# Giving out the last part of a convolution norm as a line of stages over four channel tiles

## The chip, the cores and the metric

The kernel runs on one core of one Trainium2 chip. The metric is device time in microseconds of one execution; the runs of the kernel before are given as a median of three. A core has five engines that run side by side and meet through semaphores: TensorE (PE, matrix products; its weight loads are shown as PEld), VectorE (DVE), ScalarE (ACT), GpSimd (POOL) and SyncE (SP), which here mostly issues DMAs. Each engine works through its own queue in order: an instruction that waits holds up everything behind it on that engine.

## The reference

One inference step of a one-layer streaming encoder for a prompt of 2048 tokens and a sample of 64 tokens with a cache: an input projection, then a convolution module and a chunk-band attention on the same normalised input, a gated merge, an output projection, and a SwiGLU feed-forward part. What matters here is the convolution module:

```python
def layer_norm(x, g, b):
    xf = x.astype(jnp.float32)
    mu = jnp.mean(xf, axis=-1, keepdims=True)
    var = jnp.mean(jnp.square(xf - mu), axis=-1, keepdims=True)
    y = (xf - mu) * lax.rsqrt(var + NORM_EPS)
    return (y * g.astype(jnp.float32) + b.astype(jnp.float32)).astype(x.dtype)

def conv_module(u, hist, w_dw, b_dw, ln_g, ln_b, w_out):
    ext = jnp.concatenate([hist, u], axis=1)
    y = lax.conv_general_dilated(
        ext, w_dw[:, None, :], window_strides=(1,), padding='VALID',
        dimension_numbers=('NWC', 'WIO', 'NWC'), feature_group_count=CONV_DIM)
    y = jax.nn.silu(layer_norm(y + b_dw, ln_g, ln_b))
    return y @ w_out, ext[:, -(CONV_K - 1):]
```

`...` of the layer is left out: the projection with `w_out` and the merge come in the kernel's second phase. All is computed in float32 to the accuracy of products of split numbers: an operand x is held as a high part (x rounded to the format that PE multiplies) and a low part (x minus the high part), and a product is three matmuls.

## The kernel before

**Two phases.** The first phase goes through the 2112 tokens in four blocks (576, 512, 512 and 512 tokens; the first holds the 64 sample tokens). For each block PE computes the stages q, 0, k, 1, v, 2, 3, g in this order (line 564): q, k and v are projections, 0 to 3 are the four channel tiles of the convolution's GLU input, g are the gates. The second phase merges convolution and attention (`merge`, line 1736), projects, and does the feed-forward part.

**Side work in lanes.** Only PE's order is written out by hand (line 1644); side work is written as Python generators that are resumed between PE's products. `Stream` keeps an estimate of each engine's load; every 500 ns of estimated PE time (`STEP_NS`, line 37) a tick pumps the lanes: norms, `work`, attention, `tail`, convolution taps. A generator yields an estimated time (`stream.when("act")` is the time at which ACT's queue is estimated to be done), and is not resumed before PE's estimate has reached it. Each tick resumes the lane `tail` at most once. When stage 0 of the next block begins, and again at the end of the first phase, the lanes `conv` and `tail` are drained: what is left in them is given out at once, without its times (lines 1696 to 1698 and 1710 to 1712).

**The convolution norm.** `conv_norm` (line 1296) is the generator in the lane `tail`: one for the 64 sample tokens and one for 512 prompt tokens of block 0, then one of 512 tokens for each of the blocks 1 to 3. The two of block 0 run one behind the other. It works on `y`, four channel tiles of 128 partitions. POOL adds the four tiles to `s`, PE multiplies by a matrix of 1/512 (`total`, tile `pm`), DVE subtracts the mean, ACT squares, POOL adds, PE sums again, ACT takes the square root and DVE the reciprocal. Then comes the last part: POOL multiplies the four tiles by `s` (lines 1332 to 1334), and for each tile ACT computes a tanh into a temporary `ln`, DVE computes gain and bias in place on `y` and the product with 1 + tanh, ACT copies the high part, DVE subtracts to get the low part, and SP stores both to `c_d` in DRAM, from which the second phase loads them (tile `cin`).

**Buffers.** `temp` takes one of seven buffers of the ring "t", which gates, attention, the q and k rows and the norms share. `parts` takes a pair (part_h, part_l) of rings with two buffers each (`NS = 2`, line 781), which the norm shares with `store_kq` (q and k parts, line 1038) and `finish_head` (attention's output, line 1443). A pair is free when its store has landed. `low` (line 740) would give a subtraction to POOL if that were sooner by `TT_LESS`, which is 9e9 (line 43).

At the end of the first phase its pools are closed, and the second phase's pool of tiles (line 1720) takes the same memory: a tile there, such as `t` of `merge`, waits until the old tiles under it have been read.

Of the kernel before, what the change touches and what calls it, by code (L numbers as in the profile page):

```python
# [10 lines left out]
AF = mybir.ActivationFunctionType  # L11
# [99 lines left out]
class Lane:  # L111
# [18 lines left out]
    def step(self, entry):  # L130
        try:
            got = next(entry[0])
        except StopIteration:
            self.gens.remove(entry)
            return
        entry[1], entry[2] = got if isinstance(got, tuple) else (got, {})
# [486 lines left out]
def streaming_layer(ctx: ExitStack, tc: tile.TileContext, I, O):  # L623
    nc = tc.nc
    stream = Stream()
    pe, dve, act, gps = (
        Meter(e, n, stream) for e, n in ((nc.tensor, "pe"), (nc.vector, "dve"), (nc.scalar, "act"), (nc.gpsimd, "pool"))
    )
# [43 lines left out]
    lnh = const.tile([P, 8], F32, name="lnh")  # L672
# [67 lines left out]
    def low(hi, lo, src, n, less=0.0):  # L740
        e, name = either(n, less)
        stream.after(name, "act")
        e.tensor_tensor(lo, src, hi.bitcast(F32), ALU.subtract)
        return name
# [38 lines left out]
    def temp(name, shape=(P, 512)):  # L783
        return wk.tile(list(shape), F32, tag="t", name=name, bufs=NT)

    def parts(n=None, shape=(P, 512)):
        return (
            wk.tile(list(shape), F32R, tag="sh", name="part_h", bufs=NS),
            wk.tile(list(shape), F32R, tag="sl", name="part_l", bufs=NS),
        )  # L790
# [226 lines left out]
    bias = wk.tile([P, 640], F32, name="bias")  # L1017
# [278 lines left out]
    def conv_norm(y, c0, n, t0):  # L1296
        yv = y[:, :, c0 : c0 + n]
        yield lambda: not conv.gens
        s = wk.tile([P, 512], F32, tag="ln_s", bufs=1)

        def total():
            ps = ps_g.tile([P, 512], F32, tag="gp", name="pm")
            pe.matmul(ps[:, :n], ones, s[:, :n], start=True, stop=True)
            return ps

        gps.tensor_tensor(s[:, :n], yv[:, 0], yv[:, 1], ALU.add)
        for ct in (2, 3):
            gps.tensor_tensor(s[:, :n], s[:, :n], yv[:, ct], ALU.add)
        yield stream.when("pool") + PE_LAG
        pm = total()  # L1310
        yield stream.when("pe")
        for ct in range(4):
            dve.tensor_tensor(yv[:, ct], yv[:, ct], pm[:, :n], ALU.subtract)
        yield stream.when("dve")
        act.activation(s[:, :n], yv[:, 0], AF.Square)
        for ct in range(1, 4):
            tmp = temp("ln")
            act.activation(tmp[:, :n], yv[:, ct], AF.Square)
            yield stream.when("act")
            gps.tensor_tensor(s[:, :n], s[:, :n], tmp[:, :n], ALU.add)  # L1320
        yield stream.when("pool") + PE_LAG
        pm = total()
        yield stream.when("pe")
        act.activation(s[:, :n], pm[:, :n], AF.Sqrt, bias=eps_t)
        yield stream.when("act")
        for c in range(0, n, P):
            e = min(n, c + P)
            dve.reciprocal(s[:, c:e], s[:, c:e])
            yield
        yield stream.when("dve")  # L1330
        done = []
        for ct in range(4):
            gps.tensor_tensor(yv[:, ct], yv[:, ct], s[:, :n], ALU.mult)
            done.append(stream.when("pool"))
        for ct in range(4):
            yield done[ct]
            tmp = temp("ln")
            act.activation(tmp[:, :n], yv[:, ct], AF.Tanh, bias=lnh[:, 4 + ct : 5 + ct], scale=lnh[:, ct : ct + 1])
            yield stream.when("act")
            dve.tensor_scalar(yv[:, ct], yv[:, ct], lng[:, ct : ct + 1], lnb[:, ct : ct + 1], ALU.mult, ALU.add)  # L1340
            dve.scalar_tensor_tensor(tmp[:, :n], tmp[:, :n], 1.0, yv[:, ct], ALU.add, ALU.mult)
            yield stream.when("dve")
            hi, lo = parts()
            act.activation(hi[:, :n], tmp[:, :n], AF.Copy)
            yield stream.when("act")
            name = low(hi[:, :n], lo[:, :n], tmp[:, :n], n, TT_LESS)

            def store(ct=ct, hi=hi, lo=lo):
                for l, a in enumerate((hi, lo)):
                    nc.sync.dma_start(c_d[l, ct, :, t0 : t0 + n], a[:, :n].bitcast(F32))  # L1350

            stream.at(stream.when(name), store)

    def gates(b, free):

        o = PBLOCKS[b][0]
        w = PBLOCKS[b][1] - o

        def part(g, ws, c0, c1):
            ps = columns(*ws, kts(hh), kts(hl), c0, c1)  # L1360
            t = temp("gate")
            stream.after("act", "pe")
            act.activation(t[:, : c1 - c0], ps[:, : c1 - c0], AF.Tanh, scale=0.5)
            nc.scalar.dma_start(g_d[g // 8, g % 8, :, o + c0 : o + c1], t[:, : c1 - c0])

        def pair(g):
            ws = [W.get(("in", 2560 + g * P, h)) for h in range(2)]
            return [[[w[l][:, k, e * P : e * P + P] for w in ws for k in range(4)] for l in range(2)] for e in range(2)]

        n = 16 - SPLIT_G if b + 1 < len(PBLOCKS) else 16  # L1370
        for g in range(0, n, 2):
            for e, ws in enumerate(pair(g)):
                for c in halves(0, w):
                    part(g + e, ws, *c)
                if e:
                    W.done()
                    W.done()
                yield g + e
        rest = [ws for g in range(n, 16, 2) for ws in pair(g)]
        for c0, c1 in ((0, w // 2), (w // 2, w)):  # L1380
            for i, ws in enumerate(rest):
                part(n + i, ws, c0, c1)
                if c1 == w and i % 2:
                    W.done()
                    W.done()
            free["columns"] = c1
# [261 lines left out]
    for b, stage in ORDER:  # L1648
        lo, hi = PBLOCKS[b]
# [43 lines left out]
        else:  # L1693
# [7 lines left out]
            if stage == 3:  # L1701
                if b == 0:
                    tail.add(conv_norm(y, 0, SMP, 0))
                    tail.add(conv_norm(y, SMP + HIST, QB, SMP))
                else:
                    tail.add(conv_norm(y, 0, QB, lo))
# [675 lines left out]
```

## Time and profile before

| What | Value |
|---|---|
| Median of 3 runs | 2945.97 us (2940.69, 2946.77, 2945.97) |
| Profiled execution, its own time | 2941.67 us |
| Span of the profile | 2939.5 us |
| Mean granted clock of PE | 0.997 |
| First tanh to last part of the 64-wide norm, block 0 | 272.3 to 302.3 us |
| The same, block 1 | 550.3 to 579.5 us |

The span runs from the first to the last instruction. In rows of the timeline the columns are start (us from the span's start), duration in us, engine, source line, operation, tiles written <- tiles read, shape, count, and in brackets the idle time of the engine before and what ended it. All operations are recorded in one helper, so nearly all have line 105; tiles are told apart by their names. In rows by tile there stand duration in ns (least/median/most), then the start of the first and of the last of the group. The granted clock is the share of its full clock that PE was given.

### The profile page before, as it was taken

Reading aid. Unit: us, or ns where it says so; the run is one execution under the profiler, and the core shown is the slowest. Engines: PE = TensorE matmul, PEld = TensorE weight load, DVE = VectorE, ACT = ScalarE, POOL = GpSimd, SP = SyncE. Lnnn points to the kernel's source line nnn. Section 1 sums busy time; section 2 is a strip of 40 time slices with the busy share of each in tenths; the row PEclk is TensorE's granted clock in tenths of the full one; section 3 lists DMA queues with packets and bytes.
Section 4 is the critical chain, followed back from the end, with each engine's and each line's share of the span. In section 5 each row is a group of like instructions: output and inputs, shape, how many; then the busy total and the mean of one; then the engine's idle time right before and its main releaser. Section 6 shows DMA issues by size and latency. Waiting matters only on the chain.

```text
span 2939.5 us, 44832 instructions
## 1 busy us (share of the span) xinstructions
PE 2889.3 (98%) x16193; PEld 2587.5 (88%) x16193; DVE 2053.9 (70%) x3648; ACT 1362.7 (46%) x2453; POOL 1164.9 (40%) x753
## 2 busy tenths in 40 slices
PE   7999999999999999999999999999999999999999
PEld 5899777888888887988999998999999999999998
DVE  5897788668967885577777756666666557566666
ACT  3346543751564266563444345444444345444442
POOL 1201210111011002553566452366567742465667
PEclk9999999999999999999999999999999999999999
DMA  9989899978996987984444875332333965333333
GB/s 322 315 305 314 287 281 329 285 232 306 285 297 197 320 270 224 291 295 157 144 144 146 292 261 200 97 122 94 115 115 104 346 220 179 97 103 106 115 107 127
DMA packets 467067, 628.04 MB, mean 214 GB/s; under 512 B 36196, under 2 KB 314584, under 8 KB 466845
## 3 DMA queue, kind: packets, MB, share of 16 engines
q1 hardware_dynamic: 452944, 606.11, 63.4%
q10 hardware_dynamic: 13901, 19.08, 1.9%
q8 instruction: 127, 2.08, 0.3%
q14 instruction: 95, 0.78, 0.1%
HBM read 476.53 MB, written 148.54 MB: 213 GB/s over the span
## 4 chain that ended last, share of the span: by engine, by line
PE 47%; DVE 2%; ACT 1%; DMA 1%; issue 1%; POOL 0%; SPq 0%; ACTq 0%; DVEq 0%; POOLq 0%
PE ps L105 29%; PE pd L105 13%; PE pw L105 5%; DVE wlo L105 1%; ACT whi L105 1%; DVE ps L105 0%; DMA cin<-o_d 0%; DMA x<-x_d 0%; DVE acc L105 0%; ACT xn L105 0%; DMA wst<-in_w_ffn_in 0%; DMA wfo<-in_w_ffn_out 0%; DMA tg<-g_d 0%; DVE sums L105 0%; PE pt L105 0%
## 5 line engine op out<-in xcount | busy, mean ns | idle before, releaser
L105 PE MATMUL ps<-t,whi 128*128 128x384 f32 (+1 forms) x2112 | 502.0, 322 | 2.8 <-ACT u L105 1.7
L105 POOL TENSOR_TENSOR wlo<-wst,whi 128x1024 fp32r<-128x1024 f32 (+1 forms) x159 | 362.7, 2293 | 246.1 <-ACT whi L105 214.4
L105 ACT ACTIVATE whi<-wst 128x1024 fp32r<-128x1024 f32 (+1 forms) x265 | 258.3, 979 | 316.1 <-PE ps L105 129.6
L105 PE MATMUL ps<-b,whi 128*128 128x384 f32 (+1 forms) x1584 | 380.7, 325 | 6.4 <-DVE v L105 2.1
L105 PEld LDWEIGHTS ps<-t,whi 128*128 128x128 f32 x2112 | 367.8, 188 | 10.1 <-ACT u L105 3.9
L105 DVE SCALAR_TENSOR_TENSOR y<-u,wd,y 128x512 f32<-128x512 f32 (+1 forms) x480 | 370.1, 774 | 8.0
L105 PE MATMUL ps<-hh,whi 128*128 128x512 f32 (+2 forms) x992 | 362.8, 366 | 0.1
L105 DVE TENSOR_TENSOR acc<-acc,pd 128x512 f32<-128x512 f32 x482 | 322.2, 685 | 48.1 <-PE pd L105 45.6
L105 PE MATMUL ps<-hh,wlo 128*128 128x512 f32 (+2 forms) x992 | 345.2, 348 | 0.0
L105 PE MATMUL ps<-hl,whi 128*128 128x512 f32 (+2 forms) x992 | 344.5, 347 | 0.0
L105 PE MATMUL ps<-t,wlo 128*128 128x384 f32 (+1 forms) x1056 | 338.5, 321 | 0.0
L105 PE MATMUL pd<-whi,hid 128*128 128x512 f32 x912 | 297.9, 391 | 0.6 <-DVE hid L105 0.3
L105 PEld LDWEIGHTS ps<-b,whi 128*128 128x128 f32 x1584 | 276.9, 188 | 14.6 <-DVE v L105 3.2
L105 ACT ACTIVATE pr<-pr,sm 128x640 f32<-128x640 f32 (+3 forms) x272 | 201.9, 749 | 137.1 <-DVE sm L105 134.8
L105 PE MATMUL ps<-b,wlo 128*128 128x384 f32 (+1 forms) x792 | 256.1, 323 | 0.0
L105 POOL TENSOR_TENSOR r<-t,mhalf 128x1 f32<-128x1 f32 (+2 forms) x68 | 82.3, 1219 | 403.7 <-DVE t L105 377.8
L105 PEld LDWEIGHTS ps<-hh,wlo 128*128 128x128 f32 x992 | 186.5, 188 | 22.6
L105 DVE TENSOR_TENSOR wlo<-wst,whi 128x1024 fp32r<-128x1024 f32 (+1 forms) x106 | 135.9, 1286 | 100.3 <-ACT whi L105 98.9
L105 PEld LDWEIGHTS pd<-whi,hid 128*128 128x128 f32 x912 | 171.2, 188 | 37.2 <-DVE acc L105 1.8
L105 PEld LDWEIGHTS ps<-hh,whi 128*128 128x128 f32 x992 | 187.0, 189 | 18.2 <-issue 3.3
L105 PEld LDWEIGHTS ps<-hl,whi 128*128 128x128 f32 x992 | 187.4, 189 | 14.3 <-issue 1.7
L105 PEld LDWEIGHTS ps<-t,wlo 128*128 128x128 f32 x1056 | 198.2, 188 | 0.8
(233 smaller groups left out, 6309.6 us busy)
## 6 DMA issues: line engine op xcount, KB each, us to landing
whi<-w_din_h SPq DMA_DIRECT2D x72, 512.0 KB, 6.4
wlo<-w_din_l SPq DMA_DIRECT2D x72, 512.0 KB, 7.3
wst<-sum_d SPq DMA_DIRECT2D x131, 256.0 KB, 3.1
wfo<-in_w_ffn_out SPq DMA_DIRECT2D x64, 512.0 KB, 4.1
wmod<-in_w_ada SPq DMA_DIRECT2D x46, 512.0 KB, 8.8
sum_d<-ws SPq DMA_DIRECT2D x88, 256.0 KB, 2.0
wst<-in_w_ffn_in SPq DMA_DIRECT2D x85, 256.0 KB, 3.2
wst<-in_w_in SPq DMA_DIRECT2D x40, 512.0 KB, 6.0
```

The source lines that it names most:

```text
L105: self.last = f(*args, **kw)
```

## The change

After POOL's four products the code no longer finishes one tile before it begins the next. The work of a tile is three functions: `swish` (the tanh), `times` (DVE's two operations) and `give` (high part, low part, store). They are given out as a line: step i does `give` for tile i - 2, then `times` for tile i - 1, then `swish` for tile i, in six steps for the four tiles. Ahead of each step there is one `yield`: the later of POOL's estimate for tile min(i, 3) and, from the second step on, the later of the estimates of ACT and DVE. Before there were four resumptions for each tile, with a `yield` between copy and low part, which now come in one step. The temporaries of up to three tiles are held at once. The operations themselves are unchanged.

```diff
-        for ct in range(4):
-            yield done[ct]
-            tmp = temp("ln")
-            act.activation(tmp[:, :n], yv[:, ct], AF.Tanh, bias=lnh[:, 4 + ct : 5 + ct], scale=lnh[:, ct : ct + 1])
-            yield stream.when("act")
+        tmps = [None] * 4
+
+        def swish(ct):
+            tmps[ct] = temp("ln")
+            act.activation(tmps[ct][:, :n], yv[:, ct], AF.Tanh, bias=lnh[:, 4 + ct : 5 + ct], scale=lnh[:, ct : ct + 1])
+
+        def times(ct):
+            tmp = tmps[ct]
             dve.tensor_scalar(yv[:, ct], yv[:, ct], lng[:, ct : ct + 1], lnb[:, ct : ct + 1], ALU.mult, ALU.add)
             dve.scalar_tensor_tensor(tmp[:, :n], tmp[:, :n], 1.0, yv[:, ct], ALU.add, ALU.mult)
-            yield stream.when("dve")
+
+        def give(ct):
+            tmp = tmps[ct]
             hi, lo = parts()
             act.activation(hi[:, :n], tmp[:, :n], AF.Copy)
-            yield stream.when("act")
             name = low(hi[:, :n], lo[:, :n], tmp[:, :n], n, TT_LESS)
 
-            def store(ct=ct, hi=hi, lo=lo):
+            def store():
                 for l, a in enumerate((hi, lo)):
                     nc.sync.dma_start(c_d[l, ct, :, t0 : t0 + n], a[:, :n].bitcast(F32))
 
             stream.at(stream.when(name), store)
+
+        for i in range(6):
+            yield max(done[min(i, 3)], stream.when("act", "dve") if i else 0.0)
+            for step, ct in ((give, i - 2), (times, i - 1), (swish, i)):
+                if 0 <= ct < 4:
+                    step(ct)
```

## The prediction

> **What bounds the kernel now.** I read the page's first part, then who TensorE waited for, then the stretches around its two longest stops in the first phase.
>
> ```profile
> span 2939.5 us, 44832 instructions
> PE 2889.3 (98%) x16193; PEld 2587.5 (88%) x16193; DVE 2053.9 (70%) x3648; ACT 1362.7 (46%) x2453; POOL 1164.9 (40%) x753
> ...
> PE pt L105 <- DVE kn L105: 6.1, 2, 4.0
> PE ps L105 <- DVE t L105: 5.8, 5, 3.4
> ```
>
> TensorE (PE) is busy 98% of the span, so only what stops PE, or slows its clock, counts; the convolution norm runs on ACT, DVE and POOL and matters where PE waits behind it. PE's waits are few. The longest single wait in each of the two rows shown, 4.0 and 3.4 us, stands next to a convolution norm. In the table of stretches, the columns are length, then busy time of PE, weight loads, DVE, ACT and POOL, then granted clock and DMA:
>
> ```profile
> 355.00:360.50 5.50, 1.55 (x17) 0.64 (x8) 3.81 (x8) 2.85 (x7) 0.21 (x1) 1.00 0.59 159
> 360.50:370.00 9.50, 9.49 (x36) 8.15 (x37) 6.28 (x13) 3.13 (x6) 0.00 (x0) 0.64 1.07 391
> ...
> 1164.50:1172.00 7.50, 7.30 (x48) 7.04 (x48) 5.37 (x7) 2.37 (x4) 2.39 (x1) 1.00 0.66 234
> 1172.00:1175.30 3.30, 0.01 (x1) 0.01 (x1) 0.89 (x3) 0.00 (x0) 0.00 (x0) 0.80 0.58 190
> 1175.30:1181.00 5.70, 5.70 (x22) 5.70 (x23) 3.08 (x9) 1.08 (x3) 0.00 (x0) 0.52 0.92 278
> ```
>
> After each stop the granted clock is low: 0.64 for 9.5 us and 0.52 for 5.7 us. So a stop costs its length and then 9.5 x 0.36 = 3.4 us, or 5.7 x 0.48 = 2.7 us.
>
> **The stop at 356.6 (the "start stop").** Rows of PE, DVE and ACT in order of time; the number in brackets is the idle time before and what ended it:
>
> ```profile
> 360.51 0.63 PE L105 MATMUL pt<-ident,kn 128*128 128x128 f32 x4 [3.96 <-DVE kn L105]
> ...
> 357.19 0.69 DVE L105 TENSOR_TENSOR part_l<-ln,part_h 128x512 fp32r<-128x512 f32 x1 [0.33 <-ACT part_h L105]
> 359.02 0.75 DVE L105 SCALAR_TENSOR_TENSOR part_l<-pt,gqk,part_h 128x512 fp32r<-128x512 f32 x1 [1.13 <-ACT part_h L105]
> 359.68 0.68 DVE L105 TENSOR_TENSOR kn<-kn,r 128x512 f32<-128x512 f32 x1
> ...
> 356.55 0.61 ACT L105 ACTIVATE part_h<-ln 128x512 fp32r<-128x512 f32 x1
> 358.26 0.69 ACT L105 ACTIVATE part_h<-pt,gqk 128x512 fp32r<-128x512 f32 x1 [1.10 <-DMA c_d<-part_h]
> ```
>
> PE wants kn at 356.6. DVE makes it at 359.68, because it is queued behind the low part of an earlier q tile (359.02), which waits for ACT's high part (358.26), which waits until a c_d store of the norm has landed and freed one of the two part buffers (line 781, NS = 2). The norm's last four part pairs stand in that ring ahead of q's. They stand there because block 0's 512-wide norm came so late that stage 0 of block 1 had to drain it at once (line 1698): PE enters that stage at 340.72 and POOL's four products run at 337.1 to 342.0. It was late because the 64-wide norm ahead of it in the tail lane took 30 us for its last part; PE's sum for the wide one follows directly (302.43):
>
> ```profile
> 302.43 1.13 PE L105 MATMUL pm<-s,ones 128*128 128x512 f32 x2
> 340.72 0.45 PE L105 MATMUL ps<-hh,whi 128*128 128x512 f32 x1
> L105 POOL TENSOR_TENSOR y<-y,s x4: 1090/1296/1349, 337.1 to 340.7; 128x512 f32<-128x512 f32 x4
> ...
> L105 ACT ACTIVATE ln<-y,lnh x4: 427/429/432, 272.3 to 290.4; 128x64 f32<-128x64 f32 x4
> L105 DVE TENSOR_TENSOR part_l<-ln,part_h x4: 212/226/2428, 276.4 to 302.1; 128x64 fp32r<-128x64 f32 x4
> ```
>
> **The stop at 1171.9 (the "end stop").**
>
> ```profile
> 1169.59 2.79 DVE L105 TENSOR_TENSOR part_l<-ln,part_h 128x512 fp32r<-128x512 f32 x1 [0.70 <-DMA o_d<-part_l]
> 1174.75 0.49 DVE L105 SCALAR_TENSOR_TENSOR t<-tg,ps 128x320 f32<-128x320 f32 x1 [2.38 <-DMA c_d<-part_l]
> ...
> 1175.29 0.90 PE L105 MATMUL ps<-cin,whi 128*128 128x320 f32 x2 [3.42 <-DVE t L105]
> ...
> 1166.57 0.32 SPq L1460 DMA_DIRECT2D o_d<-part_l  x1
> ...
> 1172.40 0.32 SPq L1350 DMA_DIRECT2D c_d<-part_l  x1
> 1172.81 0.38 SPq L384 DMA_DIRECT2D wst<-in_w_o  x1
> ```
>
> The merge of the second phase needs t, whose memory was the first phase's; it waits for the last c_d store of block 3's norm (issued 1172.40, t at 1174.75). PE waits for t to free PSUM. SP stands at that store too, with loads behind it.
>
> **What the change removes, adds and moves.** No instruction is added or removed: each norm keeps 8 ACT, 12 DVE operations and 8 SP stores. Sixteen resumptions (four for each channel tile) become six. How slowly they come now is in the tile's rows for block 1 and block 3 (first and last start):
>
> ```profile
> L105 ACT ACTIVATE ln<-y,lnh x4: 805/812/816, 550.3 to 573.8; 128x512 f32<-128x512 f32 x4
> L105 DVE SCALAR_TENSOR_TENSOR ln<-ln,y x4: 687/692/1464, 552.9 to 576.0; 128x512 f32<-128x512 f32 x4
> L105 ACT ACTIVATE part_h<-ln x4: 614/624/633, 555.2 to 578.1; 128x512 fp32r<-128x512 f32 x4
> L105 DVE TENSOR_TENSOR part_l<-ln,part_h x4: 692/693/694, 555.8 to 578.8; 128x512 fp32r<-128x512 f32 x4
> ...
> L105 ACT ACTIVATE ln<-y,lnh x4: 800/808/821, 1130.1 to 1163.8; 128x512 f32<-128x512 f32 x4
> ```
>
> Block 1 takes 550.3 to 579.5, 29.2 us for 16 resumptions, 1.8 us each. A new step waits for the later of two engines and carries five operations (tanh 0.81 and copy 0.62 on ACT; about 0.55 for the product, 0.69 and 0.69 on DVE), so I bound it between 1.8 and twice that, 3.6 us. Five waits and a last pair (1.3 us) give 10 to 19 us; I take 15, half of today's 30.
>
> *End stop.* Block 3's norm begins at 1130.1 and would have its last store out by about 1150 rather than 1172.4, more than 20 us before PE needs t. The next thing that could hold t is the head's o_d store, issued at 1166.57: with the 2.35 us that the last c_d store took from issue to t it is there at 1168.9, ahead of 1171.9. Saved: 3.42 + 2.74 = 6.2 us. If something else holds that memory, 0.
>
> *Start stop.* The 64-wide norm ends 15 us earlier, so the wide one's tanh moves from 341.7 to about 327 and its last part to about 342, when the drain comes at 340.7. At most one or two of its four pairs still stand ahead of q's, and kn, now 3.1 us late by its own start, is behind two pairs fewer. Saved: 3.96 + 3.42 = 7.4 us; 0 if all four are drained as now.
>
> *Clock.* The Trainium skill, page "TensorE: Matmul & The Clock Gate", section "What's actually happening", says that PE falls to half clock after an idle window of about 3.4 us and is back after about 3.4 us of work. By that each stop would cost 1.7 us behind it, and both together 10.8 us rather than 13.6; the rows show 0.64 for 9.5 us and 0.52 for 5.7 us, longer than the rule, and the sum goes by the rows.
>
> *What is added.* Copy and low part now come in one step, so DVE may stand behind ACT's copy, with attention's maxima queued behind it: at worst 0.62 us, 16 times on the wide tiles. DVE is busy 24.71 of 37 us and 27.51 of 44 us in the stretches of blocks 1 and 2, and PE hardly idle, so this is hidden; uncovered it is 10 us. Up to three tiles of the seven of the ring "t" (line 781) are held at once, and the part ring is asked for faster. Its present price in block 2:
>
> ```profile
> 545.00:582.00 37.00, 36.65 (x195) 31.10 (x194) 24.71 (x47) 25.38 (x46) 4.83 (x4) 1.00 0.95 291
> 822.00:866.00 44.00, 44.00 (x242) 37.94 (x241) 27.51 (x59) 31.80 (x60) 6.40 (x6) 1.00 0.94 293
> ...
> 848.83 0.63 ACT L105 ACTIVATE part_h<-ln 128x512 fp32r<-128x512 f32 x1 [1.38 <-DMA c_d<-part_h]
> ...
> DMA to landing us min/median/max: 2.0/5.0/9.3
> ```
>
> ACT stood 1.38 us there and PE not at all; at the start stop a like chain cost 7.4. Between 0 and 7.4 for each of the three norms of blocks 1 to 3, I take 1 us, near the row without a loss: 3 us. The stores keep their order within a norm; on SP's queue the last three of block 3 (1167.17 to 1172.40) move ahead of the loads of wst and tg, which now stand behind them, so these come earlier too. POOL's queue is not passed: the low parts stay on DVE (line 43 makes POOL's bid hopeless).
>
> **Sum.** 2941.67 (the profiled execution: span 2939.5 and 2.2 around it) - 6.2 - 7.4 + 3 = 2931.1. The three runs are 2940.69, 2946.77 and 2945.97; with the profiled one the mean is 2943.8, 2.1 above the profiled one, which lies 4.3 below the median of the three. So 2933.
>
> **Rivals.** (a) Only one stop goes, because the other's place is taken by the next late thing (at the start: q's own stores in the same ring): 2943.8 - 6.2 + 3, about 2940. (b) The norm isn't on PE's path, or the parts overlapped before: in the drained norm the trace already has all tanh within 341.7 to 344.4, so there the source's order was not the engines' order and the change does nothing in that place. Against it: the norms that aren't drained plainly come one tile in 7 to 10 us. Time 2944. (c) Slower: the two part buffers become the wait. A pair is held for 0.62 + 0.69 + about 0.4 of issue + 5.0 landing = 6.7 us, so the ring gives one tile in 3.4 us; steps under that make the third and fourth copy stand at the head of ACT's queue for up to 6.7 - 2 x 1.8 = 3.1 us, with exponentials and PSUM evictions behind it. ACT waits of 1.4 us cost nothing, the start stop's did; past about 3 us PE stops. Once in each norm of blocks 1 to 3, at 7.4: 2943.8 - 13.6 + 22.2 = 2952.4. For it: 9.3 us is the longest landing. Against: steps nearer 3 us.
>
> **Chances.** Forecast 0.48, (a) 0.17, (b) 0.12, (c) 0.23. About 0.2% (5.9 us) is what runs of this kernel can tell from no change: below 2940.1 is faster, above 2951.9 slower. All of the forecast and 0.10 of (a) are faster: 0.58. Of (c) 0.20 is slower; the rest, 0.22, is same. The range 2926 to 2952 runs from both stops gone with no new wait, a further few us less, to (c)'s middle; it leaves out half of (c) and about 0.05 below.
>
> **What would show it.** Block 3's last c_d store near 1150, and no PE wait for t; the wide norm's tanh near 327, PE's wait for kn under 1 us at stage 0 of block 1, and the clock at 1.00 in both places; norms of 10 to 19 us. Wrong, if ACT's waits for c_d landings grow past 3 us with PE stops beside them at the norms, or if PE's two stops stay under other names.

## The result, and the profile after

The changed kernel takes 2955.03 us, median of 6 runs (2951.09 to 2958.51), against 2944.61 for the kernel before (6 runs, 2940.69 to 2946.77): a ratio of 1.0038, 95% interval 1.0027 to 1.005. It is about 10 us slower where 2933 was forecast, and 3 us above the range. Its profiled execution took 2958.51 us, the longest of the six.

The first lines are the span and then TensorE's waits after (total, times, longest):

```profile
span 2956.6 us, 44837 instructions
PE pt L105 <- DVE kn L105: 7.4, 2, 5.2
PE pt L105 <- DVE x_t L105: 7.1, 3, 4.2
...
PE ptp L105 <- ACT pr L105: 2.9, 3, 2.4
PE ps L105 <- DVE t L105: 2.3, 6, 0.8
```

The wait for t is down from 3.4 us to 0.8, as forecast. The wait for kn has grown, from 4.0 to 5.2, and two rows that did not matter before are new: x_t (the rows of block 1's norm tiles) and pr (the softmax). The table of stretches shows where the loss arises (length, busy PE, weight loads, DVE, ACT, POOL, then granted clock and DMA):

```profile
316.30:320.60 4.30, 0.09 (x2) 0.06 (x1) 0.83 (x2) 0.00 (x0) 3.40 (x3) 0.78 1.04 396
320.60:326.00 5.40, 5.40 (x16) 4.45 (x17) 1.78 (x8) 2.02 (x6) 0.00 (x0) 0.54 1.07 388
326.00:331.20 5.20, 2.77 (x13) 1.93 (x11) 3.97 (x12) 5.20 (x12) 0.73 (x1) 1.00 1.06 321
331.20:336.00 4.80, 4.79 (x18) 4.04 (x19) 4.80 (x13) 2.06 (x4) 1.62 (x1) 0.64 0.45 145
...
362.30:367.60 5.30, 0.06 (x2) 0.04 (x1) 1.53 (x4) 2.28 (x5) 0.00 (x0) 0.57 0.73 231
367.60:374.00 6.40, 6.40 (x22) 4.77 (x23) 2.02 (x6) 2.49 (x6) 0.00 (x0) 0.55 1.01 288
```

Between 316 and 336 us, where the kernel before hardly stopped, PE stands 4.2 and 2.4 us and runs behind the stops at 0.54 for 5.4 us and at 0.64 for 4.8 us: 4.2 + 2.5 + 2.4 + 1.7 = 10.8 us. At the first stop POOL is the engine that works while PE is still (3.40 of 4.30 us). POOL's and DVE's rows after, each in order of time:

```profile
311.89 3.77 POOL L105 TENSOR_TENSOR y<-y,s 128x512 f32<-128x512 f32 x3 [9.33 <-DVE pl L105]
315.62 2.35 POOL L105 TENSOR_TENSOR wlo<-wst,whi 128x1024 fp32r<-128x1024 f32 x1
317.94 1.26 POOL L105 TENSOR_TENSOR y<-y,s 128x512 f32<-128x512 f32 x1
319.15 0.55 POOL L105 TENSOR_TENSOR r<-t,mhalf 128x1 f32<-128x1 f32 x1
...
328.55 0.73 POOL L105 TENSOR_TENSOR r<-t,mhalf 128x1 f32<-128x1 f32 x1 [8.84 <-DVE t L105]
...
314.67 0.15 DVE L105 TENSOR_SCALAR t<-ssq 128x1 f32<-128x1 f32 x1
319.74 0.75 DVE L105 TENSOR_SCALAR x_t<-x_t,r 128x1024 f32<-128x1024 f32 x1 [4.92 <-POOL r L105]
```

The norm tile's sum is there at 314.82 (314.67 + 0.15). Its reciprocal root r is one POOL instruction of 0.55 us, and it runs at 319.15, because the wide convolution norm's four products y<-y,s and a low part of weights (2.35 us) stand ahead of it on POOL. DVE is idle for 4.92 us until r comes, then scales x_t, and PE can transpose. At the second stop POOL had been idle for 8.84 us when the next tile's sum came, so there the sum itself was late. It follows from the first stop: ACT squares that tile at 326.57, behind an exponential (325.85) that had stood 2.86 us for its maximum, and that maximum waited for PE's scores, which came only at 324.02. About 1.1 us more are the wide norm's own operations on DVE, which stand ahead of x_t (r is there at 329.28, x_t starts at 330.40). Before the change the same r was waited for by nobody for long; its sum was ready at 313.84, and it ran at once:

```profile
313.92 0.55 POOL L105 TENSOR_TENSOR r<-t,mhalf 128x1 f32<-128x1 f32 x1 [0.28 <-DVE sm L105]
```

The stop for kn is still there. Rows after, of PE, ACT and SP's queue:

```profile
367.59 1.08 PE L105 MATMUL pt<-ident,kn 128*128 128x128 f32 x4 [5.25 <-DVE kn L105]
...
350.39 0.62 ACT L105 ACTIVATE part_h<-ln 128x512 fp32r<-128x512 f32 x1
365.37 0.69 ACT L105 ACTIVATE part_h<-pt,gqk 128x512 fp32r<-128x512 f32 x1 [1.48 <-DMA c_d<-part_h]
...
352.86 0.32 SPq L479 DMA_DIRECT2D wlo<-w_dqkv_l  x1
355.20 0.32 SPq L1354 DMA_DIRECT2D c_d<-part_h  x1
358.47 0.32 SPq L1354 DMA_DIRECT2D c_d<-part_l  x1
```

The norm's last high part is finished at 351.0, eleven us before PE wants kn (367.59 less 5.25), but SP issues its store only at 355.20, behind weight loads, and the low part's at 358.47; q's copy waits until 365.37 for the landing of the first, ten us after its issue. The DMA engines are full until then (shares of 1.02 from 355 to 360 us and 1.00 from 362.3 to 365.4). DVE's low part of q, and kn behind it, come after that copy, as before the change.

At the end of the phase, rows of SP's queue, DVE and PE:

```profile
1167.17 0.32 SPq L1354 DMA_DIRECT2D c_d<-part_l  x1
...
1190.81 0.49 DVE L105 SCALAR_TENSOR_TENSOR t<-tg,ps 128x320 f32<-128x320 f32 x1 [0.68 <-DMA o_d<-part_l]
...
1176.07 0.47 PE L105 MATMUL ptp<-ident,pr 128*128 128x128 f32 x1 [2.44 <-ACT pr L105]
```

and the stretch behind that stop:

```profile
1176.10:1180.00 3.90, 3.65 (x14) 3.06 (x15) 1.75 (x3) 2.42 (x4) 0.00 (x0) 0.50 0.46 139
```

The same matmuls stand some 16.7 us later here than before, so the last c_d store, at 1167.17, would be at 1150.5 by the old clock, where 1150 was forecast and 1172.40 it was, and t waits 0.68 us for the head's o_d store. In exchange the last softmax is late: PE stands 2.44 us for pr, and the clock behind it costs 3.9 x 0.50 = 2.0 us more in the first 3.9 us alone.

Adding up over cells of 2.5 us of the same table (idle: length less busy PE; clock: busy PE times what the granted clock lacks, where it is under 0.97) gives what PE lost in each part of the first phase, in us, for the kernels of this document. The differences of these sums are the measure in what follows; they leave out a few us per kernel which show in the medians and not in PE's stops. Each is of one profiled execution, which can lie some us from the median: 3.5 above it for the changed kernel, 2.9 below for the one before, 6.6 below for prod_dve.

Each ratio is to the runs of before that were taken with that kernel.

| kernel | 255–400 | 400–520 | 520–1100 | 1100–1215 | median, us | ratio to before |
|---|---|---|---|---|---|---|
| before | 10.3 | 4.1 | 1.0 | 8.7 | 2944.61 | |
| after | 21.8 | 7.7 | 1.3 | 8.8 | 2955.03 | 1.0038 [1.0027, 1.005] |
| line_64wide | 17.0 | 6.2 | 1.9 | 9.5 | 2955.64 | 1.0039 [1.0027, 1.0052] |
| line_123 | 9.8 | 3.5 | 1.4 | 9.6 | 2942.5 | 1.0001 [0.9992, 1.001] |
| line_wide0 | 9.7 | 5.9 | 1.3 | 8.4 | 2948.05 | 1.0021 [1.0012, 1.003] |
| line_3 | 10.8 | 3.7 | 1.3 | 7.8 | 2943.74 | 1.0002 [0.9993, 1.0011] |
| wide_held | 8.6 | 9.7 | 1.7 | 7.2 | 2948.5 | 1.0013 [1.0004, 1.0022] |
| prod_dve | 6.6 | 18.7 | 1.7 | 7.7 | 2959.98 | 1.0053 [1.0041, 1.0066] |
| early_tile | 11.0 | 2.1 | 1.1 | 7.7 | 2943.64 | 0.9998 [0.9989, 1.0007] |
| prod_dve_lag | 6.6 | 6.3 | 5.9 | 7.4 | 2951.31 | 1.0026 [1.0013, 1.0038] |
| before_lag | 10.4 | 6.9 | 6.8 | 8.7 | 2952.0 | 1.0025 [1.0016, 1.0035] |
| line_3_slow | 12.6 | 2.6 | 1.4 | 6.0 | 2944.33 | 0.9996 [0.9987, 1.0005] |
| prod_dve_lag1 | 6.6 | 11.5 | 1.6 | 7.0 | 2953.74 | 1.0039 [1.0025, 1.0053] |
| tile_dve | 10.8 | 9.8 | 1.2 | 7.7 | 2947.22 | 1.0011 [1.0002, 1.002] |

After against before: +11.5 at the start, +3.6 in the next stretch, +0.3 and +0.1: 15.5 us of the 17.1 between the two profiled spans. The medians differ by 10.4 us only, so the sizes given here are those of these two executions. The profiled execution of line_64wide lies 0.5 us from its median and has the same two stops for x_t, so they are no accident of one execution.

### The profile page after: what moved, and what is told of

Its sections match the earlier page's. It is cut to its first block, busy times and chain, and to the rows that moved or that the text cites. A ratio compares the mean times of both kernels' runs of the same rounds, so it can differ in the third digit from the quotient of the medians.

```text
span 2956.6 us, 44837 instructions
## 1 busy us (share of the span) xinstructions
PE 2895.5 (98%) x16193; PEld 2590.2 (88%) x16193; DVE 2047.7 (69%) x3648; ACT 1363.5 (46%) x2453; POOL 1165.0 (39%) x753
```

## The experiments

**Which norm costs it.** Four kernels give out only some of the five norms as a line; the other norms run one tile at a time.

```diff
+        if not (t0 == 0):            # line_64wide; t0 > SMP: line_123; t0 == SMP: line_wide0
+            for ct in range(4):      # t0 == PBLOCKS[3][0]: line_3
+                yield done[ct]
+                swish(ct)
+                yield stream.when("act")
+                times(ct)
+                yield stream.when("dve")
...
+            return
         for i in range(6):
```

> Only the 64-wide norm of block 0 is given out as a line of stages; the four 512-wide norms go one tile at a time as before. Theory T: the loss arises because the shorter 64-wide norm lets block 0's wide norm begin its products some 25 us earlier, on POOL ahead of the row scales r of block 1's norm tiles; so this one edit alone costs 8 to 15 us (2953 to 2960 against 2945 before), with TensorE waits for x_t of 3 us and more near 320 and the wait for kn still there. Rival R (copy and low part in one step, with two part buffers, hold ACT and DVE in every wide norm): under 3 us from before, since no wide norm is changed. Rival N (every change of order re-times the attention, with no pattern by norm): some 5 us in either direction.

> Only the norms of blocks 1 to 3 are given out as a line; both norms of block 0 as before. Theory T: nothing is lost up to 380 us, the stop for kn near 360 is there as before (about 4 us), and the time is 2938 to 2947, since the stop for t near 1172 goes (6 us) but may be eaten by a new one. Rival R: slower by 5 to 15 us, in equal shares beside the norms near 565, 845 and 1150. Rival N: 5 us in either direction.

> Only block 0's 512-wide norm is given out as a line; the 64-wide one and blocks 1 to 3 as before. Theory T: the wide norm comes as late as before and is drained at stage 0 of block 1, so the time stays within 4 us of before (2941 to 2949) and the stop for kn stays at 3 to 5 us. Rival R: 2 to 6 us slower. Rival N: 5 us in either direction.

> Only block 3's norm is given out as a line. Theory T: the program is the same as before up to about 1100 us, and the stop for t near 1172 (3.4 us and 2.7 us of clock) goes; if nothing takes its place 2937 to 2941, if the new stop for pr that the changed kernel has near 1176 belongs to this norm too, 2943 to 2948. Rival R: slower by 2 to 5 us. Rival N: 5 us in either direction.

The line in the 64-wide norm alone costs as much as the whole change, 2955.64 us (1.0039), and PE's rows there show the two stops for x_t:

```profile
320.67 1.11 PE L105 MATMUL pt<-ident,x_t 128*128 128x128 f32 x4 [4.22 <-DVE x_t L105]
330.80 1.09 PE L105 MATMUL pt<-ident,x_t 128*128 128x128 f32 x4 [2.66 <-DVE x_t L105]
```

The stop for kn, expected to stay, is gone in that kernel, and PE waits 2.6 us for a weight load near 380 in its place. The line in blocks 1 to 3 costs nothing (1.0001), which is against the rival that copy and low part in one step, or the two part buffers, hold the engines up. Nor does it bring anything. PE's rows in line_123:

```profile
360.46 0.63 PE L105 MATMUL pt<-ident,kn 128*128 128x128 f32 x4 [3.98 <-DVE kn L105]
...
1160.37 0.47 PE L105 MATMUL ptp<-ident,pr 128*128 128x128 f32 x1 [2.44 <-ACT pr L105]
```

The start stop is as before, and at the end the stop for t has been exchanged for the one for pr; line_3 has the same 2.44 us. So it is throughout: the seven kernels of the table with this line in block 3's norm have a stop for pr of 2.44 or 2.45 us, and the six that finish one tile at a time there have a stop for t of 3.4 us. The wide norm of block 0 alone costs 0.2%, at the edge of what was expected, and PE's lost time rises only between 400 and 520.

**The early place of the wide norm.** In the changed kernel that norm is held back to about its old place.

```diff
         yield lambda: not conv.gens
+        if t0 == SMP:
+            yield stream.load["pe"] + 15000.0
         s = wk.tile(
```

> The changed kernel (a line in all five norms), but block 0's 512-wide norm may only begin 15 us (of TensorE's planned work) after the 64-wide one has ended, so that it comes about when it came before the change. Theory T (the loss comes from that norm's early place among block 1's norm tiles): TensorE's waits for x_t near 320 and 331 fall from 6.7 us to under 1 us, the stop for kn stays at 3 to 5 us, and the time is 2941 to 2950. Rival D (the line's dense steps, wherever the norm stands): 2951 to 2958.

Its tanh now runs at 344.2 to 347.9 us (before: 341.7 to 344.4). No stop for x_t is left, the one for kn is 2.96 us, the start costs 8.6 us rather than 21.8, and the time is 2948.5. So the dense steps themselves cost little there; the place did. What remains over before is a new stop 70 us later, with its reason in DVE's row (SP had issued the large loads wmod at 417.14, ahead of bias at 419.45):

```profile
428.50 0.29 DVE L105 CUSTOM_DVE_ANT_0 pr<-sc,bias 128x128 f32<-128x128 f32 x1 [3.29 <-DMA bias<-rb_d]
...
428.85 0.80 PE L105 MATMUL sc<-kk,q 128*128 128x256 f32 x2 [5.27 <-DVE sm L105]
```

**POOL's queue or DVE and ACT.** In prod_dve the norm stays early, but its four products leave POOL. In early_tile there is no line at all, and the 64-wide norm ends early because it is resumed once for each tile.

```diff
+            if t0 == SMP:                                  # prod_dve
+                dve.tensor_tensor(yv[:, ct], yv[:, ct], s[:, :n], ALU.mult)
+                done.append(stream.when("dve"))
...
```

```diff
                 swish(ct)                                  # early_tile: the loop of before
-                yield stream.when("act")
+                if t0:
+                    yield stream.when("act")
...
```

> The changed kernel, but the four products y*s of block 0's 512-wide norm run on DVE rather than POOL, at the same early place. Theory TP (what makes x_t late is POOL's queue: r waits behind the four products and a low part of weights): the stop for x_t near 320 (4.2 us) is under 1 us and the second near 331 (2.4 us) goes with it as its consequence; time 2943 to 2949. Rival TD (it is the norm's work on DVE and ACT among the norm tiles): the stops for x_t stay at 4 us or more in all, 2950 to 2958.

> The kernel before (one tile at a time, no line anywhere), but the 64-wide norm of block 0 is resumed once for each tile rather than four times, so that it ends as early as in the changed kernel. By the order of the program, r of one norm tile then stands behind one product of the wide norm and r of the next behind the other three. Theory T: the loss comes with the early place and needs no line: stops for x_t between 310 and 345 of 2 us or more, 2948 to 2957. Rival L (the overlap of the line's stages is what costs): no stop for x_t, 2941 to 2946.

POOL's and PE's rows in prod_dve:

```profile
316.58 0.93 POOL L105 TENSOR_TENSOR r<-t,mhalf 128x1 f32<-128x1 f32 x1 [1.36 <-DVE t L105]
...
325.43 0.63 PE L105 MATMUL pt<-ident,x_t 128*128 128x128 f32 x4 [0.71 <-DVE x_t L105]
```

With the norm at its early place and the line kept, r runs as soon as t is there, and the stop for x_t is 0.71 us. The start costs 6.6 us, 3.7 less than in the kernel before, since the stop for kn has gone too. This is the local gain that the prediction hoped for. The whole kernel is nevertheless slower than the changed one, 2959.98 us, where 2943 to 2949 was expected; the next experiment is about that.

In early_tile, POOL's rows:

```profile
316.05 1.09 POOL L105 TENSOR_TENSOR y<-y,s 128x512 f32<-128x512 f32 x1 [5.68 <-DVE sm L105]
317.10 0.55 POOL L105 TENSOR_TENSOR r<-t,mhalf 128x1 f32<-128x1 f32 x1
317.62 4.03 POOL L105 TENSOR_TENSOR y<-y,s 128x512 f32<-128x512 f32 x3
322.13 0.56 POOL L105 TENSOR_TENSOR r<-t,mhalf 128x1 f32<-128x1 f32 x1 [0.48 <-DVE t L105]
```

The expectation for it failed: I took the three products ahead of the second r for a wait, but that tile's sum was ready only when they had ended. There is no stop for x_t and the time is 2943.64, like before. The products begin at 316.05 here, 4.2 us later than in the changed kernel, and the first r runs between them. So it is not an early place as such, but r behind the products, that costs. The line itself is neither enough for the stop nor needed in the wide norm: prod_dve keeps the line and has no such stop, line_64wide has the stop without a line in that norm.

**Where prod_dve's gain goes.** Rows of prod_dve, of DVE and PE and then of SP's queue:

```profile
432.23 0.29 DVE L105 CUSTOM_DVE_ANT_0 pr<-sc,bias 128x128 f32<-128x128 f32 x1 [7.52 <-DMA bias<-rb_d]
432.58 0.80 PE L105 MATMUL sc<-kk,q 128*128 128x256 f32 x2 [8.13 <-DVE sm L105]
...
413.19 0.33 SPq L1474 DMA_DIRECT2D o_d<-part_h  x1
418.56 0.33 SPq L1474 DMA_DIRECT2D o_d<-part_l  x1
...
421.09 1.99 SPq L249 DMA_DIRECT2D wmod<-in_w_ada  x4
423.13 1.11 SPq L1487 DMA_DIRECT2D bias<-rb_d  x2
```

In the kernel before, bias was issued ahead of these loads:

```profile
409.45 1.09 SPq L1473 DMA_DIRECT2D bias<-rb_d  x2
416.62 2.43 SPq L249 DMA_DIRECT2D wmod<-in_w_ada  x4
```

SP stands 5 us at an o_d store, and then four large loads go out ahead of the small one that the attention needs. Three runs hold wmod back:

```diff
+        lag = 8000.0 if self.stream.load["pe"] > 300000.0 else 0.0   # lag1: 300000 < load < 365000
-        self.stream.at(self.stream.when("pe"), lambda n=self.given: self.free(n), True)
+        self.stream.at(self.stream.when("pe") + lag, lambda n=self.given: self.free(n), True)
```

> The kernel of the run prod_dve, with one thing more: after 300 us of planned work a used wmod buffer is given out again 8 us later, so that SP issues the bias loads of the next two heads ahead of four wmod loads, as in the kernel before, and not behind them. In prod_dve TensorE was 7 us ahead of before at 398 us and lost 8.1 us at 432.6, where DVE waited for bias. Theory S (the second part of the loss is SP's order: loads for the attention stand behind wmod): the stop at 432 is under 1 us, and the time is 5 to 12 us below prod_dve's, 2940 to 2950. Rival B (the lead is lost anyway, since the transfers of this stretch are the bound): another stop of 5 us or more for a load between 400 and 500, time above 2951.

> The kernel before with the later wmod loads alone, as a measure of what that edit does by itself. Both theories: within 4 us of before (2940 to 2948), with the stop for kn near 360 as before; faster than 2940 would say that the wmod loads hold up the attention's in the kernel before too.

> The kernel of the run prod_dve_lag, but only the wmod group that SP issues near 417 us in the kernel before is held back by 8 us, not the later ones, which cost 7 us and more in the run before_lag. Theory S (SP's order of loads is the second part of the loss): the stops near 470 and 750 are those of before, the stop at 430 is about 3 us, and the time is 2937 to 2946, in reach of before. Rival B (the lead is lost anyway): above 2950.

In prod_dve_lag, bias goes out ahead of wmod, and PE's stop is 3.19 us rather than 8.13; under 1 us was expected. Near 490 the same holds for kk. Rows of prod_dve, and then of prod_dve_lag:

```profile
495.37 1.41 PE L105 MATMUL sc<-kk,q 128*128 128x320 f32 x4 [4.14 <-DMA kk<-k_d]
...
477.34 4.81 SPq L249 DMA_DIRECT2D wmod<-in_w_ada  x4
485.27 0.45 SPq L1444 DMA_DIRECT2D kk<-k_d  x1
```

```profile
480.07 0.60 SPq L1445 DMA_DIRECT2D kk<-k_d  x1
...
483.94 7.51 SPq L249 DMA_DIRECT2D wmod<-in_w_ada  x4
```

There the second stop is gone. PE loses 6.3 us between 400 and 520 rather than 18.7, and the time falls by 8.7 us, to 2951.31, 1 us above the range that the order of SP's loads gave. The rival's time is met (above 2951) and its stop isn't: none of 5 us is left. The edit costs 7 us by itself (before_lag, 2952.0: the modulation's sums wait for their late wmod), so prod_dve_lag takes no longer than its own control, and if the two costs add, nothing of prod_dve's loss is left. That before_lag would stay within 4 us was wrong. prod_dve_lag1 was to keep the gain without that price and did not: its stop near 430 is 3.00 us, but the next wmod group (477 us in prod_dve, 473 here) is not held back, kk stands behind it again (3.93 us) and the time is 2953.74, in the rival's range. That stop is the one which the order of SP's loads would give; that no order of them keeps all of the lead is not excluded.

**Early, on DVE, without a line.**

```diff
# early_tile and prod_dve together
```

> No line anywhere; the 64-wide norm is resumed once for each tile (as in early_tile), and block 0's 512-wide norm has its four products on DVE. Theory TP: no stop for x_t, and the stop for kn near 360 goes as it did in prod_dve, so TensorE is 4 us or more ahead of before at 400 us; the time is 2934 to 2942 if nothing takes the lead away again, and 2943 to 2956 with a stop of 3 us or more for bias or kk between 415 and 500 if SP's order of loads does (theory S). Rival L (the line's overlap is what removed the stop for kn): the stop for kn stays above 3 us.

No stop for x_t, and the stop for kn has gone, but a row of the same place takes its turn: PE waits 3.52 us for a low part (ptp behind part_l) at 363.52, and the start costs 10.8 us, no less than before, so the lead of 4 us that was expected at 400 us isn't there. Later 5.75 us are lost at 434 for the softmax that waits for bias. 2947.22 us is in the branch in which SP's loads take the lead away, though here the lead was hardly there.

**The end.** In line_3 the line's steps in block 3's norm are spread a little.

```diff
-            yield max(done[min(i, 3)], stream.when("act", "dve") if i else 0.0)
+            yield max(done[min(i, 3)], stream.when("act", "dve") + 1000.0 if i else 0.0)
```

> The kernel of the run line_3 (a line in block 3's norm alone), with each of the line's steps 1 us later, so that the norm ends near 1157 to 1160 rather than 1151, and its last c_d store still comes ahead of t. Theory E (the stop for pr that took the place of the stop for t comes from the dense steps, which push the last softmax back): the stop for pr near 1160 falls from 2.4 us to under 1 us, t is not waited for, and the time is 2937 to 2943. Rival F (the last softmax stands bare once the norm ends before it, however it is spaced): a stop of 2 us or more for pr stays, 2941 to 2947.

```profile
1159.56 1.20 PE L105 MATMUL ptp<-ident,pr 128*128 128x128 f32 x9 [1.61 <-ACT pr L105]
```

The stop for pr falls to 1.61 us and the clock stays at 1.00 behind it; PE loses 6.0 us in that stretch rather than 8.7. This lies between the two theories, and the time, 2944.33, can't be told from before. The edit also did not end the norm where it should have, near 1157 to 1160: three of its tiles are out early, but the last step comes only at the end of the phase, its low part runs at 1167.92 and its last store goes out at 1169.63, so t waits for it again (1.53 us on DVE, 1.01 on PE). What goes along with the stop for pr is the place of the last scores in PE's order: they start at 1152.59 in the kernel before (PE then waits 0.50 us for pr), at 1154.70 in line_3_slow (1.61) and at 1156.53 in line_3 (2.44), where 0.8 us later PE has nothing left but to wait. The code gives out scores only while DVE's planned queue is short (`SCORE_ROOM`), which the dense steps fill; that this is what moves them is argued, not shown, and whether the last softmax would stand bare with any early norm stays open. None of the twelve kernels is faster than the one before by more than its interval.

## Why the prediction was wrong, step by step

*The failed step* is "POOL's queue is not passed: the low parts stay on DVE". It looked for what the change puts on POOL and found nothing, but the change moves what is there: the wide norm's four products ran at 337.1 to 342.0 before and run at 311.9 to 319.2 after, because the 64-wide norm ahead of it in the tail lane ends earlier. I had worked out that move and counted it as a gain alone. At the new place r is queued behind the products, and x_t and PE wait for r. It costs 10.8 us in the profiled execution, and taking the products off POOL takes this away (prod_dve). Beside the terms of the sum: the start stop, put at -7.4, came to +0.7; the end stop, put at -6.2, to +0.1; the new waits, put at +3, to +0.3; and 10.8 and 3.6 us (between 400 and 520) came that the sum did not have, together the 15.5 us of the table.

*The start stop.* That the wide norm's tanh would move to about 327 was right:

```profile
327.80 1.51 ACT L105 ACTIVATE ln<-y,lnh 128x512 f32<-128x512 f32 x2
```

Its last part was to end about 342 and ended at 351.7, and the saving of 7.4 us turned into a stop of 5.25 us and 6.4 x 0.45 = 2.9 us of clock. Two of the norm's pairs still stood ahead of q's, as the step had allowed for. But it took the pair's end for the end of the wait; the buffer comes free when the store has landed, and that store stood on SP and in full DMA engines until 365.

*The end stop.* The mechanism was right: the last store is issued 22 us earlier by the old clock, t no longer waits for it, and o_d comes next, as the prediction said. The saving of 6.2 us was paid back by the stop for pr (2.44 us, and 2.0 and more of clock). The step asked what else could hold t's memory, not what an earlier norm does to the order of the last scores.

*The new waits,* 3 us for the norms of blocks 1 to 3: about nothing (line_123). Rival (c), the two part buffers as the wait, falls with it; that its time, 2952.4, comes near the measured one is luck. ACT's waits for c_d in the norms of all blocks are 2.5 us in four pieces after. Nor does the length of ACT's wait decide: at the start stop before the change it was 1.10 us, less than the 1.38 us that cost nothing in block 2.

*The norms' length,* 10 to 19 us: block 0's 64-wide norm, on which the start hangs, takes 14.2 us (273.5 to 287.7), near the 15 of the forecast. Block 1's takes 23.6 us from the first tanh to the end of the last low part (565.4 to 588.3 and 0.7). By the prediction's own count, five waits and a last pair of 1.3 us, a wait is 4.5 us, over the upper bound of 3.6.

```profile
L105 ACT ACTIVATE ln<-y,lnh x4: 804/805/807, 565.4 to 577.6; 128x512 f32<-128x512 f32 x4
L105 DVE TENSOR_TENSOR part_l<-ln,part_h x4: 683/688/693, 572.4 to 588.3; 128x512 fp32r<-128x512 f32 x4
```

*The second part of the loss,* 3.6 us between 400 and 520, was not foreseen in kind. In the changed kernel it is mostly a wait for kk (1.7 us, at 500.1), one for a softmax (1.9 us, at 505.8) and the slow clock behind them. SP has issued two wmod groups (470.97 and 481.51) ahead of that kk (489.11), where before the change it issued one (469.84). That is like the wait that prod_dve_lag removes; no run removes it in the changed kernel itself.

## What to carry to other kernels

A change that makes one thing shorter moves all that is queued behind it: list, for each engine, what the moved instructions now stand in front of, above all the one short instruction (here 0.55 us on POOL) for which another chain waits. A buffer's wait ends when the store out of it lands, so on a full DMA the last issue and its queue decide, not the compute (here the landing came ten us behind the issue). In this kernel, where TensorE is 98% busy and the order is planned from estimates, a stop that was removed came back at a later transfer in wide_held, prod_dve and tile_dve; look for that transfer's place in its queue before the saving is counted.

## What the runs showed of the hardware

The slow clock behind a stop was not a matter of the stop's length alone. Stops of 4.21 and 5.25 us were followed by 0.54 for 5.4 us and 0.55 for 6.4 us, and of 2.44 us in two places by 0.64 for 4.8 us and 0.50 for 3.9 us, but the stop of 2.53 us in prod_dve left the clock at 1.00, and so did one of 3.19 us in prod_dve_lag (426.5 to 429.7 us, and 1.00 up to 434). The rows of prod_dve:

```profile
325.50:329.05 3.55, 1.02 (x7) 0.60 (x7) 3.47 (x8) 2.52 (x6) 1.96 (x1) 1.00 1.05 340
329.05:333.00 3.95, 3.36 (x14) 2.47 (x15) 3.95 (x11) 1.91 (x3) 0.24 (x1) 1.00 1.00 255
```

Nor does the clock fall where the stop ends. After the changed kernel's second stop PE works again from 331.21; the granted clock is 1.00 from 331.2 to 332.0, 0.50 from 332.4 to 335.4 and 1.00 from 335.8. So it is halved for about 3.4 us, and from about 1.1 us after the stop.

The Trainium skill, page "TensorE: Matmul & The Clock Gate", section "What's actually happening", puts the fall behind an idle window of about 3.4 us, and says that the window runs freely. The length of the slow stretch, 3.4 us, agrees. That the same length falls once on the one side and once on the other would go with a free window; that a stop of 2.44 us, with 1.1 us of work between it and the fall, is enough does not go with a window that is idle throughout. An estimate from these figures: if such windows follow one another, the one that ended with the fall went from 328.9 to 332.3 and held 2.3 us of the stop, so a window idle for two thirds would do, and a longer stop that is cut in two by a window's end would not. No run here was made to test that.
